# Where the low part of the mixer's weights comes from: a subtraction on GpSimd, or a DMA that adds

## The chip, the core and the metric

One core of a Trainium2 chip runs one inference step of a hybrid decoder layer. The metric is the device time of one execution in microseconds (us). TensorE (PE) multiplies matrices, VectorE (DVE), ScalarE (ACT) and GpSimd (POOL) work element by element, SyncE (SP) only issues DMAs. GpSimd and ScalarE can issue DMAs as well.

## The reference, cut to what matters

The layer is a half-step feed-forward block, a mixer, and a second half-step block, in float32, for 512 prompt tokens and 32 sample tokens (544 columns):

```
x = x + 0.5 * swiglu(rms(x), w_ffn1_gu, w_ffn1_down)
u = rms(x) @ w_in                      # one projection for everything below
o_a = dilated window attention of u's q, k, v   # 12 heads, 3 groups
o_b = gated delta rule of u's q, k, v           # 8 heads, causal convolution before, chunked form
x = x + (sigmoid(gA) * (o_a @ w_proj_a) + sigmoid(gB) * (o_b @ w_proj_b)) @ w_out
x = x + 0.5 * swiglu(rms(x), w_ffn2_gu, w_ffn2_down); y = rms(x)
```

What this case touches is only how the weights of `w_in` come to TensorE, not what is computed with them.

## The kernel before, in words

**Precision.** TensorE reads a short form of float32 (`fp32r`). So each operand is split in two: `hi` is the value rounded to that form, `lo` what is left, value - hi. A product is made of three matmuls, hi x hi, hi x lo and lo x hi, which add up in one PSUM bank.

**Weights.** All weight matrices are cut into 1896 tiles of 128 x 128, laid out in DRAM in the order in which they are used (`Plan`, `in_W_dram`). Four tiles are a group; two groups are a chunk of 512 KB. `load_raw` (line 401) brings a chunk into one of two `raw` buffers; in the mixer it does so from GpSimd's queue (`RQ="gpsimd"`), in the feed-forward blocks from SyncE's. `split_next` (line 424) makes a group out of half a chunk, in a tile `G` of shape 128 x 2 x 512: ScalarE copies `raw` into the first half (`hi`, rounding it), then VectorE or GpSimd writes raw - hi into the second half (`lo`). GpSimd does so in the mixer, except where the unit under way is of kind `pa` or `pb`. `prefetch` (line 457) is called before each unit and splits up to four groups ahead, as far as there are free slots. The mixer has four slots of tag `G`: a column of eight tiles takes two, so while one column is used the next one is made, in the slots of the one before.

**Units.** The program is a list of units (`make_plan`), each a column of up to eight weight tiles times one half of the tokens (272 columns of activations): 24 matmuls (`unit`, line 582) into one PSUM bank `mm`, two units for a column. Within a tile the matmuls are hi x `xh`, hi x `xl`, lo x `xh`; so the third matmul of a unit is the first that needs `lo`. After a unit's matmuls its results are taken out by VectorE (multiplied by the token's 1/rms), and by ScalarE where a tanh follows.

**The mixer.** Its units are the projections: `gdn` (convolution and delta rule, 24 columns), `at` (attention, 36 columns), `z` and `gate`. They are 76 pairs of groups, 152 groups in all. Among them run side chains, written as generators: the causal convolution (tiles `U` and `y`; three VectorE steps y = U * w + y over 568 columns, with a ScalarE step before and a tanh after them), the delta rule for pairs of heads, the attention per slot, and the sample tokens. GpSimd also works for these: small copies of the ends of `U` into `convout`, products of 128 x 512 for the delta rule, and clearing of tiles.

**What sets the order.** The program is written in one order for all engines, and each engine runs its own instructions in that order. A planner decides where the steps of the side chains go: `Meter` keeps an estimate of when each engine gets through what it was given, and `pump` (line 620), called after each weight tile of a unit, issues the side steps that it holds ready. An instruction of GpSimd or a DMA on its queue is counted there with a duration of its own, and a matmul is held to start when its `G` tile is ready.

Of the kernel before, what the change touches and what calls it, by code (L numbers as in the profile page):

```python
# [13 lines left out]
AF = mybir.ActivationFunctionType  # L14
ALU = mybir.AluOpType
AX = mybir.AxisListType

P = 128
# [19 lines left out]
CFG = dict(S=62, S2=4, G=4, G2=8, RAW=2, U3=3, H=10, HM=6, LA=4, LAG=3.0, SLACK=0.0, BANKS=3, PRE=3, LOV=("pa", "pb"), CV=0, WARM=4, EP=8, DUE=2, RES=0, RQ="gpsimd")  # L38
# [7 lines left out]
class Meter:  # L46
    """An estimate of when each engine gets through what it was given, in us.
    It only decides in which order independent work is issued."""
# [77 lines left out]
class Plan:  # L126
    """Order in which the 128 x 128 weight tiles are used; host and chip follow it."""
# [16 lines left out]
def stagger(n, tail, head=0):  # L144
    """(tile, half) order: the first `head` and the last `tail` tiles go half by half."""
    out = [(i, h) for h in range(2) for i in range(head)]
    for i in range(head, n - tail):
        out += [(i, 0), (i, 1)]
    out += [(i, h) for h in range(2) for i in range(n - tail, n)]
    return out  # L150
# [53 lines left out]
def consts():  # L204
    """Arrays that depend on shapes alone: identity, masks and distances."""
# [53 lines left out]
class Builder:  # L259
# [20 lines left out]
    def room(self, keeps):  # L280
        """Tiles that the delta-rule chains under way will still ask for."""
        return max([v for v in self.rest.values() if keeps or v < 16], default=0)

    def need(self, n, keeps=False, room=None, spare=0):
        """Wait, in the order of issue, until n tiles of the common pool are free."""
# [4 lines left out]
    def until(self, ok):  # L290
        """The side chains go on until something holds."""
# [29 lines left out]
    def ring(self, tag, bufs, t):  # L321
        """A tile waits for the one whose place it takes."""
# [65 lines left out]
    def rsqrt(self, out, v, tmp, steps):  # L388
        """out = v ** -0.5 by a shifted exponent and Newton steps."""
# [34 lines left out]
    def split_next(self, ui, pool=None):  # L424
        """Bring the next group of weight tiles in as hi + lo if a slot is free."""
# [19 lines left out]
        self.tt(t[:, 1, :], src, t[:, 0, :], ALU.subtract, self.nc.gpsimd if pool else None)  # L445
# [101 lines left out]
    def xw_tile(self, n, h, which):  # L547
        """x * w as hi + lo; the tokens' 1/rms is applied to the products."""
# [10 lines left out]
    def norm_fin(self, h):  # L559
        """1/rms of one half of the tokens, on all partitions."""  # L560
# [38 lines left out]
    def step(self, g):  # L599
        """One step of a side chain; it says what its next step waits for."""  # L600
# [15 lines left out]
    def pump(self):  # L616
        """Issue what the side chains have ready."""
# [18 lines left out]
    def force(self):  # L636
        """The chain that can go on first goes on."""
# [31 lines left out]
    def run_d(self):  # L669
        """Norms whose sums had time to come together."""  # L670
# [37 lines left out]
    def after_x(self, n, h, which):  # L708
        """The n-th tile of the residual is final: prepare what the next norm needs."""
# [78 lines left out]
    def z_fin(self, n, h, z, t):  # L788
        """A head's output, gated, as hi + lo."""
# [13 lines left out]
    def z_load(self, n):  # L803
        """The output of head n, once it is there."""
# [8 lines left out]
    def fin_a(self):  # L813
        """The attention's heads as hi + lo."""
# [94 lines left out]
    def gating(self):  # L909
        """beta, log decay, its sums within a chunk and their exponentials.  # L910
        Columns: h * 4 + chunk, then two for the sample rows (head of four, sequence, step)."""
# [78 lines left out]
    def token_norms(self, ss, k, cols, bk):  # L990
        """ss [128, 2, k]: sums of squares of q and k.  Returns 1/|q| * dk^-0.5 (k columns),
        beta/|k|^2, that times the decay to the chunk's end, |k|."""
# [225 lines left out]
    def stack(self, a, parts):  # L1218
        """Rows (head, 32) of a, as hi (0) and lo (1), with the parts one above the other: [part, 32], head."""
# [189 lines left out]
    def attn_slot(self, j):  # L1409
        """The prompt rows of slot j.  The group without dilation has its tokens in order (a tile of  # L1410
# [383 lines left out]
```

## Time and profile before

| | us |
|---|---|
| median of three runs | 1734.32 |
| the three runs | 1730.17, 1735.02, 1734.32 |
| span of the profiled execution, which is its own time to 0.1 us | 1730.2 |
| TensorE busy in the span | 1656.1 |
| VectorE, ScalarE, GpSimd busy | 1072.3, 573.1, 373.4 |
| mixer (first to last mixer unit, about) | 425 to 1110 |

The profile is one execution. Its table by stage gives for each stretch of time what each engine was busy; what is missing to the stretch's length is idle time. Its waits say on whom an engine waited. A row of the timeline merges neighbouring equal instructions (x2, x3); its first number is the start in us from the span's beginning. In TensorE's rows of a unit, a row of two `xh` matmuls begins with lo x `xh` of one weight tile and goes on with hi x `xh` of the next.

### The profile page before, as it was taken

The page shows a single profiled execution, that of the slowest core. Times are in us where ns is not written, and L with a number is a line of the kernel's source. Part 1 is how long each engine was busy: PE and PEld are TensorE (multiplying, and loading weights), DVE is VectorE, ACT ScalarE, POOL GpSimd, SP SyncE. Part 2 cuts the span into 40 slices and gives each one's busy share as a digit, 9 for nine tenths or more (in the row PEclk, how much of TensorE's full clock was granted, in tenths as well). Part 3 has the DMA queues.
Part 4 walks back from the last instruction along what each step waited for, and adds up shares of the span by engine and source line. Part 5 has one row for each costly group of instructions (what it writes and reads, how often), then busy time and mean ns, then how long its engine had stood idle before and what let it go on. Part 6 is the DMA issues. An engine that isn't in the chain of part 4 may idle for free.

```text
span 1730.2 us, 33573 instructions
## 1 busy us (share of the span) xinstructions
PE 1656.1 (96%) x13373; PEld 1607.8 (93%) x13373; DVE 1072.3 (62%) x2508; ACT 573.1 (33%) x1356; POOL 373.4 (22%) x441
## 2 busy tenths in 40 slices
PE   8999999999988999999899899999999999999997
PEld 7999999999988888888889788999999999999996
DVE  7754255545879869789958665344456654255534
ACT  5332223332332324343333244333233323223332
POOL 5000000011545534454425233420011000000012
PEclk9999999999999999999999999999999999999999
DMA  5223222322333455446347666332243222223221
GB/s 177 87 85 98 86 86 86 98 85 75 111 100 115 135 180 185 135 156 193 117 137 238 171 219 182 123 119 89 86 139 97 84 89 87 97 74 98 86 75 63
DMA packets 116434, 205.13 MB, mean 119 GB/s; under 512 B 30962, under 2 KB 57108, under 8 KB 116276
## 3 DMA queue, kind: packets, MB, share of 16 engines
q1 hardware_dynamic: 104708, 162.43, 29.2%
q0 software_dynamic: 10992, 39.99, 7.7%
q8 instruction: 105, 1.72, 0.4%
q10 hardware_dynamic: 576, 0.56, 0.1%
q14 instruction: 53, 0.43, 0.1%
HBM read 172.20 MB, written 30.73 MB: 117 GB/s over the span
## 4 chain that ended last, share of the span: by engine, by line
PE 73%; DVE 20%; DMA 3%; ACT 2%; issue 2%; SPq 1%; POOL 0%; DVEq 0%; ACTq 0%
PE sd L120 40%; PE mm L120 32%; DVE y L120 4%; DVE Yc L120 3%; DVE inv L120 2%; DVE H L120 1%; DVE nrm L120 1%; DVE ast L120 1%; DVE av L120 1%; DVE s L120 1%; DVE R L120 1%; DMA md<-ast 1%; DVE U L120 1%; DVE kq L120 1%; DVE r L120 1%
## 5 line engine op out<-in xcount | busy, mean ns | idle before, releaser
L120 PE MATMUL mm<-xh,G 128*128 128x272 f32 x3632 | 753.7, 297 | 21.6 <-DVE smp L120 10.4
L120 PEld LDWEIGHTS mm<-xh,G 128*128 128x128 f32 x3632 | 596.6, 192 | 42.5 <-issue 26.5
L120 PE MATMUL mm<-xl,G 128*128 128x272 f32 x1816 | 530.0, 292 | 0.5 <-DVE xl L120 0.4
L120 PE MATMUL sd<-xh,G 128*128 128x272 f32 x1904 | 363.4, 288 | 0.0
L120 PEld LDWEIGHTS mm<-xl,G 128*128 128x128 f32 x1816 | 349.2, 192 | 1.4 <-DVE xl L120 0.6
L120 ACT ACTIVATE G<-raw 128x512 fp32r<-128x512 f32 x474 | 273.3, 619 | 178.6 <-PE mm L120 111.6
L120 PEld LDWEIGHTS sd<-xh,G 128*128 128x128 f32 x1904 | 300.5, 188 | 0.2
L120 POOL TENSOR_TENSOR G<-raw,G 128x512 fp32r<-128x512 f32 x158 | 217.3, 1391 | 322.7 <-ACT G L120 303.0
L120 PE MATMUL sd<-xl,G 128*128 128x272 f32 x952 | 273.8, 288 | 0.0
L120 DVE TENSOR_TENSOR G<-raw,G 128x512 fp32r<-128x512 f32 x316 | 204.7, 690 | 70.9 <-ACT G L120 66.7
L120 POOL TENSOR_TENSOR acc<-acc,H 128x272 f32<-128x272 f32 x55 | 44.7, 814 | 911.5 <-ACT H L120 908.1
L120 PEld LDWEIGHTS sd<-xl,G 128*128 128x128 f32 x952 | 179.0, 188 | 0.1
L120 PE MATMUL sd<-hh,G 128*128 128x272 f32 x1287 | 163.0, 288 | 0.0
L120 PEld LDWEIGHTS sd<-hh,G 128*128 128x128 f32 x1287 | 161.8, 188 | 0.1
L120 ACT ACTIVATE H<-H 128x272 f32<-128x272 f32 (+1 forms) x105 | 45.1, 429 | 193.4 <-DVE H L120 193.4
L120 ACT ACTIVATE hh<-H 128x272 fp32r<-128x272 f32 x88 | 38.0, 431 | 202.0 <-DVE H L120 202.0
L120 PE MATMUL mm<-hh,G 128*128 128x272 f32 x825 | 104.7, 288 | 0.0
L120 PEld LDWEIGHTS mm<-hh,G 128*128 128x128 f32 x825 | 103.8, 188 | 0.0
L120 DVE SCALAR_TENSOR_TENSOR y<-U,vec,y 128x568 f32<-128x568 f32 x72 | 94.2, 1308 | 7.8 <-ACT y L120 6.0
L120 DVE SCALAR_TENSOR_TENSOR H<-H,H 128x272 f32<-128x272 f32 x120 | 55.2, 460 | 26.3 <-ACT H L120 25.8
L120 DVE SCALAR_TENSOR_TENSOR x<-sd,x 128x272 f32<-128x272 f32 x49 | 21.4, 439 | 77.9 <-PE sd L120 77.9
L120 DVE TENSOR_TENSOR hh<-H,hh 128x272 fp32r<-128x272 f32 x88 | 38.9, 442 | 43.8 <-ACT hh L120 43.8
(257 smaller groups left out, 1853.3 us busy)
## 6 DMA issues: line engine op xcount, KB each, us to landing
raw<-in_W_dram SPq DMA_DIRECT2D x161, 512.0 KB, 3.6
raw<-in_W_dram POOLq DMA_DIRECT2D x76, 512.0 KB, 4.0
qkv<-qd SPq DMA_DIRECT2D x36, 256.0 KB, 5.4
st<-in_ssm_dram SPq DMA_DIRECT2D x32, 256.0 KB, 4.5
cache<-in_kc_dram SPq DMA_DIRECT2D x28, 256.0 KB, 5.2
cache<-in_vc_dram SPq DMA_DIRECT2D x28, 256.0 KB, 4.3
qd<-av SPq DMA_DIRECT2D x24, 256.0 KB, 4.2
out_dram<-av SPq DMA_DIRECT2D x24, 256.0 KB, 3.8
```

The costliest lines, as they stand in the source:

```text
L120: r = f(*args, **kw)
```

## The change

In the mixer `split_next` no longer subtracts. ScalarE, after writing `hi`, writes -hi into the `lo` half; then a DMA from GpSimd's queue loads the group's raw weights from DRAM a second time (128 x 512 float32, 256 KB) and adds them onto -hi in place. The `raw` buffer is then read by ScalarE alone. Outside the mixer nothing changes (`DL` is `"mix"`). The rest of the diff removes comments and docstrings.

```
-CFG = dict(S=62, S2=4, G=4, G2=8, RAW=2, ...
+CFG = dict(DL="mix", S=62, S2=4, G=4, G2=8, RAW=2, ...
...
         self.act(t[:, 0, :], src, AF.Copy)
         if pool is None:
             pool = self.in_mix and self.units[ui][0] not in CFG["LOV"]
-        self.tt(t[:, 1, :], src, t[:, 0, :], ALU.subtract, self.nc.gpsimd if pool else None)
+        if CFG["DL"] == "all" and ui >= CFG["EP"] or self.in_mix:
+            self.act(t[:, 1, :], t[:, 0, :], AF.Copy, scale=-1.0)
+            self.nc.gpsimd.dma_start(t[:, 1, :], self.A["in_W_dram"][c][:, o:o + GRP * P], accum_op=ALU.add)
+        else:
+            self.tt(t[:, 1, :], src, t[:, 0, :], ALU.subtract, self.nc.gpsimd if pool else None)
```

GpSimd's queue, near the mixer's start, before: two subtractions, the next raw load, two more, a raw load, the copies of the convolution's ends.

```order
L120 TENSOR_TENSOR G_4915<-raw_4511,G_4915 128x512
L120 TENSOR_TENSOR G_4918<-raw_4511,G_4918 128x512
L120 DMA raw_4921<-in_W_dram 128x1024
L120 TENSOR_TENSOR G_4987<-raw_4824,G_4987 128x512
L120 TENSOR_TENSOR G_4990<-raw_4824,G_4990 128x512
L120 DMA raw_4993<-in_W_dram 128x1024
L120 COPY convout_4653<-U_4950 128x3
L120 COPY convout_4653<-U_4950 128x24
```

The same place after: each subtraction is a DMA into `G`, and the second pair stands behind the copies.

```order
L120 DMA G_4919<-in_W_dram 128x512
L120 DMA G_4923<-in_W_dram 128x512
L120 DMA raw_4927<-in_W_dram 128x1024
L120 COPY convout_4653<-U_4962 128x3
L120 COPY convout_4653<-U_4962 128x24
L120 DMA G_5010<-in_W_dram 128x512
L120 DMA G_5014<-in_W_dram 128x512
L120 DMA raw_5018<-in_W_dram 128x1024
```

The copies were put ahead of the second pair, and every subtraction became an issue of a DMA.

ScalarE at the same place, before (`y` from `U` is the convolution's first step, `U` from `y` its tanh, `G` from `raw` a split):

```order
L120 ACTIVATE G_4918<-raw_4511 128x512
L120 ACTIVATE G_4987<-raw_4824 128x512
L120 ACTIVATE G_4990<-raw_4824 128x512
L120 ACTIVATE U_4856<-y_4913 128x568
L120 ACTIVATE y_5016<-U_4950,vec_79 128x568
L120 ACTIVATE G_5071<-raw_4921 128x512
L120 ACTIVATE G_5074<-raw_4921 128x512
```

And after (`G` from `G` is -hi):

```order
L120 ACTIVATE y_4917<-U_4860,vec_79 128x568
L120 ACTIVATE G_4919<-raw_4511 128x512
L120 ACTIVATE G_4919<-G_4919 128x512
L120 ACTIVATE G_4923<-raw_4511 128x512
L120 ACTIVATE G_4923<-G_4923 128x512
L120 ACTIVATE U_4860<-y_4917 128x568
L120 ACTIVATE y_5008<-U_4962,vec_79 128x568
L120 ACTIVATE G_5010<-raw_4828 128x512
L120 ACTIVATE G_5010<-G_5010 128x512
```

The second pair of splits moved from ahead of the tanh to behind it and behind the next convolution's first step, and each split is two instructions.

ScalarE in the plain run of gate units near the mixer's end, before (`gate` is the tanh that takes out a unit, `oh` a split of the attention's output):

```order
L120 ACTIVATE gate_13471<-gate_13471 128x272
L120 ACTIVATE oh_13481<-oA_13409 128x512
L120 ACTIVATE gate_13471<-gate_13471 128x272
L120 ACTIVATE G_13507<-raw_13370 128x512
L120 ACTIVATE G_13510<-raw_13370 128x512
```

And after:

```order
L120 ACTIVATE gate_13483<-gate_13483 128x272
L120 ACTIVATE oh_13493<-oA_13432 128x512
L120 ACTIVATE gate_13483<-gate_13483 128x272
L120 ACTIVATE G_13519<-raw_13385 128x512
L120 ACTIVATE G_13519<-G_13519 128x512
L120 ACTIVATE G_13523<-raw_13385 128x512
L120 ACTIVATE G_13523<-G_13523 128x512
```

Here nothing moved; the pair of splits became four instructions behind the same tanh.

## Rows read from the trace of the kernel before

**Rows 1.** Table by stage: length, busy us per engine, clock, DMA share, GB/s

```profile
core 0 of [0], span 1730.2 us
core 0: us, PE busy (x) PEld busy (x) DVE busy (x) ACT busy (x) POOL busy (x), PEclk, DMA share, GB/s
0.00:425.00 425.00, 416.17 (x3253) 412.86 (x3254) 233.95 (x448) 139.43 (x292) 35.90 (x42) 0.99 0.29 94
425.00:560.00 135.00, 119.11 (x863) 116.00 (x862) 111.28 (x263) 38.75 (x95) 64.86 (x72) 0.92 0.35 114
560.00:860.00 300.00, 278.69 (x2372) 259.18 (x2371) 256.60 (x708) 111.04 (x308) 134.55 (x171) 0.98 0.50 156
860.00:1020.00 160.00, 148.78 (x1346) 134.68 (x1346) 107.62 (x330) 51.29 (x159) 60.82 (x71) 0.98 0.57 179
1020.00:1110.00 90.00, 85.79 (x723) 79.04 (x722) 49.25 (x132) 36.61 (x96) 33.11 (x36) 0.96 0.65 198
1110.00:1150.00 40.00, 40.00 (x322) 40.00 (x321) 12.60 (x29) 15.98 (x38) 19.35 (x20) 1.00 0.28 92
```

**Rows 2.** TensorE's waits, 425 to 1110 us: who for whom, us, times, longest

```profile
PE mm L120 <- DVE smp L120: 10.4, 3, 5.1
...
PE mm L120 <- ACT G L120: 3.4, 1, 3.4
PE sd L120 <- ACT r L120: 3.4, 1, 3.4
...
PE mm L120 <- POOL G L120: 1.4, 2, 0.8
...
PE mm L120 <- DVE inv L120: 0.2, 1, 0.2
```

**Rows 3.** Instructions on tile raw, 425 to 1110 us: ns min/median/max; landings

```profile
L120 ACT ACTIVATE G<-raw x138: 612/616/651, 434.0 to 1107.5; 128x512 fp32r<-128x512 f32 x138
L120 POOL TENSOR_TENSOR G<-raw,G x138: 1260/1292/1927, 434.7 to 1109.0; 128x512 fp32r<-128x512 f32 x138
L120 POOL DMA_DIRECT2D raw<-in_W_dram x68: 551/562/602, 438.1 to 1098.8; - x68
...
DMA to landing us min/median/max: 3.7/4.1/13.0
```

**Rows 4.** Instructions on tile y: ns min/median/max, first and last start

```profile
L120 DVE SCALAR_TENSOR_TENSOR y<-U,vec,y x72: 792/1516/2996, 434.1 to 853.3; 128x568 f32<-128x568 f32 x72
```

**Rows 5.** Timeline of VectorE at 517 us: start, us, instruction

```profile
516.85 4.32 DVE L120 SCALAR_TENSOR_TENSOR y<-U,vec,y 128x568 f32<-128x568 f32 x3 [0.97 <-ACT y L120]
```

**Rows 6.** Timeline of GpSimd at 517 us

```profile
517.36 3.21 POOL L120 TENSOR_TENSOR G<-raw,G 128x512 fp32r<-128x512 f32 x2 [1.17 <-ACT G L120]
```

**Rows 7.** DMAs of the attention's cache, 256 KB each, and their landing

```profile
L120 SPq DMA_DIRECT2D cache<-in_kc_dram x28: 327/422/1755, 604.8 to 1047.4; - x28
L120 SPq DMA_DIRECT2D cache<-in_vc_dram x28: 365/425/906, 619.4 to 1079.4; - x28
...
DMA to landing us min/median/max: 2.8/4.7/7.9
```

**Rows 8.** The page's DMA issues: count, KB each, median us to landing

```profile
raw<-in_W_dram SPq DMA_DIRECT2D x161, 512.0 KB, 3.6
raw<-in_W_dram POOLq DMA_DIRECT2D x76, 512.0 KB, 4.0
```

**Rows 9.** Timeline of ScalarE in the gate units

```profile
1113.22 1.14 ACT L120 ACTIVATE G<-raw 128x512 fp32r<-128x512 f32 x2
```

**Rows 10.** Timeline of TensorE in the gate units

```profile
1118.48 0.42 PE L120 MATMUL mm<-xh,G 128*128 128x272 f32 x2
```

**Rows 11.** Timeline of ScalarE at 770 us

```profile
770.67 1.13 ACT L120 ACTIVATE G<-raw 128x512 fp32r<-128x512 f32 x2
```

**Rows 12.** Timeline of TensorE at 772 us

```profile
772.69 0.40 PE L120 MATMUL mm<-xh,G 128*128 128x272 f32 x1 [0.84 <-POOL G L120]
```

## What the change will do to the time

> **What bounds the kernel now.** I read the page first, then one table by stage, the waits of TensorE, and then single tiles and stretches. The stages before 425 us and after about 1150 us are the two feed-forward blocks. They are untouched, and TensorE is nearly gapless there: 416.2 of 425 us [rows 1]. Everything happens in the mixer, from 425 to 1110 us. There TensorE is busy 119.1 of 135, 278.7 of 300, 148.8 of 160 and 85.8 of 90 us, so it stands idle for 15.9 + 21.3 + 11.2 + 4.2 = 52.6 us [rows 1]. The granted clock is 0.92, 0.98, 0.98 and 0.96 in these four stretches. A mean below 1 means that part of the time TensorE ran at 1.2 instead of 2.4 GHz; the loss is 0.08 x 135 + 0.02 x 300 + 0.02 x 160 + 0.04 x 90 = 23.6 us. It comes where TensorE had stood idle: the stretch with the largest idle share, 12%, has the lowest clock, and in 1110 to 1150 us, without idle time, it is 1.00 [rows 1]. So a us of idle time in the mixer goes with 23.6 / 52.6 = 0.45 us of lost clock, and I multiply every change of idle time by 1.45.
>
> What ends these waits is mostly VectorE: 18 rows of the table of waits name it, from 10.4 us down to 0.2 us, in sum 39 us; ScalarE ends 7.5 us outside the weights (four rows, the largest 3.4 us). The weights themselves end few: "POOL G" 1.4 us, "ACT G" 3.4 us [rows 2]. So the split of the weights is now nearly hidden, and the mixer is paced by TensorE with VectorE close behind, busy 111 of 135 us and 257 of 300 us in the first two stretches [rows 1].
>
> **What goes.** GpSimd's subtraction, 152 times in the mixer. One lasts 1260 ns at the least and 1292 ns as a median [rows 3]. GpSimd is not a bound, but VectorE suffers beside it: the three-input step on y takes 792 ns at the least, 1516 ns as a median and up to 2996 ns [rows 4]. At 516.85 us three of them take 4.32 us where three times the least would be 2.4 us; GpSimd's pair of subtractions at 517.36 us lies inside, and takes 3.21 us in place of twice 1.26 [rows 5, 6]. Each holds up the other. Summed over the 247 VectorE instructions of the mixer that overlap a subtraction, each against the shortest of its own form, that is 98 us of VectorE time, the largest part of it y. How much of it TensorE sees: for each of its waits on VectorE or ScalarE I took the smaller of the wait and of the stretching inside VectorE's unbroken run just before. The sum is 34 us, the upper end; the lower end is 0, as another input may be late next (a transfer, or ScalarE with its new work). I take 20 us, nearer the upper end, since in most of these waits the stretching exceeds the wait.
>
> The Trainium skill says the same of this conflict: its page "SBUF — State Buffer", section "SBUF: two separate sides", calls the port pair of the two engines an exclusive lock held for a whole instruction. The trace agrees with 792 against 2996 ns [rows 4]. The same page warns that GpSimd, locked out, can't write the descriptors of its own DMAs either; by that, the new transfers would start late where VectorE is busiest, and the slow landing among the rivals would gain weight. The issuing instruction itself shows nothing of it: 551 to 602 ns in 68 cases [rows 3].
>
> **What comes: ScalarE.** One more pass per group, -hi from hi, at the cost of a split: 616 ns [rows 3]. 152 of them are 94 us on an engine that is busy 38.8 of 135 us and 111.0 of 300 us [rows 1]. It is in order, so what stands behind a pair of groups (tanh of the convolution, copies out of PSUM) comes up to 1.2 us later; most of that lies beside VectorE's y, which is longer. I price it at nothing. If that cover fails, what it can cost is bounded by 4 waits of 1.2 us each, 5 us, since four rows of waits on ScalarE are there now.
>
> The planner, too, now counts -hi and a transfer, so the side steps stand elsewhere among the units: one pair of splits that stood ahead of a tanh on ScalarE now stands behind it and behind the next convolution's first step. The list of units stays. What this can do lies within the 39 + 7.5 us of waits on side steps [rows 2]; I set it at nothing, and keep a tenth of them, 5 us, to either side.
>
> **What comes: the transfer.** A 256 KB load with an addition, from GpSimd's queue, in place of 1.3 us of arithmetic. On GpSimd it stands where the subtraction stood, and it waits for ScalarE as that did; behind it in the queue stand the next raw load and the two small copies of U, which were held just as long before. No row shows a transfer that adds. Nearest rows: loads of 256 KB from SyncE's queue land in 2.8 us at the least and 4.7 us as a median, 7.9 at most, in the crowded middle [rows 7]; 512 KB from GpSimd's queue take 3.7, 4.1 and 13.0 us [rows 3]; over the whole run 512 KB take 3.6 us by SyncE and 4.0 by GpSimd [rows 8], so GpSimd's queue costs 0.4 us more. Below: 2.8 + 0.4 = 3.2 us, an addition for free. Above: 5.5 us, twice the 2.8 us. I take 4.3 us: the adding transfer has to read both the weights and -hi, 512 KB, so the 512 KB row (4.1 us) is nearest, and I add 0.2 us for the addition, an estimate.
>
> The Trainium skill has a price of its own, in "DMA: Bandwidth & Descriptors", section "Anatomy of one DMA": 2.0 us and the bytes at 436 GB/s, which is 2.6 us for 256 KB, an estimate that counts no addition. For the plain 512 KB load it gives 3.2 us, and the trace 3.7 at the least [rows 3], so it is low here.
>
> **Who has to wait.** A column of eight weight tiles is two groups. ScalarE begins the first split of a pair at a time H, when it is through with the last work on the unit before; the third matmul of the unit that uses the pair is the first that reads lo. With the change the first lo lands at H + 2 x 0.62 (hi, -hi) + 0.2 (two handovers) + L, thus H + 1.44 + L; the second group's at H + 2.7 + L, but it is wanted 1.5 us later, so the first decides. In the plain run of gate units H is 1113.22 us and the matmul at 1118.48 us, 5.26 us later [rows 9, 10]. In the worst pair it is 770.67 and 772.69 us, 2.02 us [rows 11, 12]. Over the 76 pairs of the mixer (H from ScalarE's rows, units counted through at 24 matmuls): 13 have 2.0 to 4.75 us, 13 have 5.27 to 5.73 us, 50 have more. With L = 4.3 the need is 5.74 us: the first 13 are short by 29 us in sum, the next 13 by 4 us, together 33 us. With L = 3.2 it is 15 us, with 3.7 it is 21 us, with 5.5 it is 69 us. Some of the 13 are late only because ScalarE waited for a stretched y; taking that stretching out of H shortens the 33 us by 5 us.
>
> **Sum.** Idle time: + 33 - 5 - 20 = + 8 us, with the clock 1.45 x 8 = + 12 us. The profiled execution has a span of 1730.2 us [rows 1], which is the lowest of the three runs; the median, 1734.3 us, lies 4 us above. So 1742 us on the profile's scale and 1746 us as a median.
>
> **Rivals.**
> Hidden transfer, on the other side: L is 3.2 to 3.7 us, the loss 15 to 21 us less 3 us, and VectorE's relief the full 34 us. Idle time changes by 18 - 34 = -16 us at 3.7 us and by 12 - 34 = -22 us at 3.2 us; times 1.45, from 1734.3 us, that is 1711 to 1702 us. For it speaks the 2.8 us row; against it that raw loads of GpSimd never landed under 3.7 us. It decides from L below about 3.9 us together with relief above 25 us. The Trainium skill's formula above (2.6 us) would end beyond it: 10 us of loss less 3 us and 34 us, times 1.45, 1695 us.
>
> A wash: relief and loss within 4 us of each other, 1734 us. That needs L near 4 us, or relief near 28 us; both are well inside the bounds.
>
> Slow landing: adding is as slow as two transfers one after the other, or the crowded middle (DMA share 0.50 to 0.65 [rows 1], to which the change adds 152 x 256 KB = 40 MB) pushes the median beyond 5 us. With L = 5.5: 69 - 9 - 20 = + 40 us, times 1.45 = + 58 us, 1792 us. Even the gate units would then wait, 1.7 us for each column.
>
> That the change does not do what it says: the order of the built program has the 152 DMAs on GpSimd's queue and 152 more passes on ScalarE, so this is left without a chance.
>
> **How the numbers follow.** About 0.3% (5 us) can be told from no change. Forecast (L from 4.0 to 5.2 us, 1740 to 1770 us): 0.39. Slow landing: 0.15. Hidden transfer: 0.28. A wash: 0.18. Slower by over 0.3% thus 0.54, the same 0.18, faster 0.28. The range 1712 to 1786 us leaves out the far half of the hidden transfer and most of the slow landing, about 0.2. The forecast's own range is 1740 to 1770 us.
>
> **What would show it.** Right: the landing of G's DMA at 4 to 5 us; y near 0.8 us in all 72 cases; TensorE's waits on a DMA into G at 25 to 40 us, most of them in 425 to 560 and after 1020 us; its waits on VectorE down from 39 to about 20 us; a clock of 0.92 or lower in 425 to 560 us. Wrong: landing under 3.7 us, or no waits on G at all, or y as long as before, in which case the subtraction was not what stretched it.

## The result and the profile after

The changed kernel takes **1827.0 us** in the median (1818.8 to 1830.9), the kernel before 1733.1 on the same chip. The ratio is 1.053, interval 1.050 to 1.056: slower by 92 us. The forecast, 12 us slower, had the sign; the size is more than seven times that, and beyond its range.

The table by stage of the changed kernel (length, busy us per engine, clock, DMA share, GB/s):

```profile
core 0 of [0], span 1817.0 us
core 0: us, PE busy (x) PEld busy (x) DVE busy (x) ACT busy (x) POOL busy (x), PEclk, DMA share, GB/s
425.00:560.00 135.00, 119.75 (x886) 114.93 (x887) 91.70 (x286) 63.22 (x134) 48.52 (x81) 0.97 0.80 191
560.00:860.00 300.00, 252.60 (x2054) 230.79 (x2054) 191.86 (x627) 126.59 (x328) 87.12 (x138) 0.92 0.69 182
860.00:1020.00 160.00, 140.85 (x1182) 127.75 (x1181) 90.53 (x319) 57.99 (x149) 44.90 (x71) 0.88 0.69 185
1020.00:1110.00 90.00, 77.55 (x620) 71.07 (x618) 35.00 (x115) 44.15 (x109) 25.87 (x37) 0.94 0.85 237
1110.00:1200.00 90.00, 76.04 (x632) 70.21 (x632) 33.48 (x93) 40.42 (x94) 18.44 (x25) 0.92 0.66 166
1200.00:1240.00 40.00, 34.72 (x264) 33.19 (x265) 10.91 (x25) 19.78 (x39) 13.69 (x18) 1.00 0.69 146
```

Against [rows 1], TensorE stands idle for 15.25 + 47.40 + 19.15 + 12.45 + 13.96 + 5.28 = 113.5 us from 425 to 1240 us, where it was 52.8 us. The lost clock is 0.03 x 135 + 0.08 x 300 + 0.12 x 160 + 0.06 x 90 + 0.08 x 90 = 59.8 us, where it was 23.6. Together that is 97 us more; the profiled spans differ by 86.8 (the clock is given to two places, which is 4 us either way here). The mixer now ends behind 1200 us, so the last two stretches count. The first stretch, where much was expected, is no worse than before; 560 to 860 us is.

TensorE's waits in 415 to 1240 us (who for whom, us, times, longest; `mm` and `sd` are the PSUM tiles that the matmuls write):

```profile
PE mm L120 <- DMA G<-in_W_dram: 50.9, 38, 8.7
PE sd L120 <- DMA cache<-in_kc_dram: 20.6, 5, 7.9
PE sd L120 <- DMA qkv<-qd: 10.2, 1, 10.2
PE sd L120 <- DVE srz L120: 6.7, 2, 4.1
PE sd L120 <- DVE av L120: 4.0, 3, 2.1
```

A DMA ended 0.8 us of TensorE's waits in the kernel before; now it is 87 us, all such rows added. But only 51 of them are waits on the new transfer; 36 are waits on the attention's cache, on `qkv` and on a state of the delta rule (20.6 + 10.2 + 2.9 + 2.2), loads that the change doesn't touch. The rows of VectorE add up to 20.3 us in 425 to 1110 us, where [rows 2] had 39.1.

The step on `y` (ns min/median/max), against [rows 4]:

```profile
L120 DVE SCALAR_TENSOR_TENSOR y<-U,vec,y x72: 769/810/2535, 430.7 to 892.7; 128x568 f32<-128x568 f32 x72
```

The median is down from 1516 to 810 ns. The new transfer, its issue on GpSimd (ns) and its landing (us):

```profile
L120 POOL DMA_DIRECT2D G<-in_W_dram x152: 844/861/940, 432.1 to 1235.7; - x152
...
DMA to landing us min/median/max: 3.6/5.6/9.8
```

And the page's DMA issues (count, KB, median us to landing), against [rows 8]:

```profile
raw<-in_W_dram SPq DMA_DIRECT2D x161, 512.0 KB, 3.6
G<-in_W_dram POOLq DMA_DIRECT2D x154, 256.0 KB, 5.7
raw<-in_W_dram POOLq DMA_DIRECT2D x76, 512.0 KB, 7.0
```

The page counts 154 new transfers: 152 for what GpSimd subtracted, two for groups that VectorE had subtracted. Of all the rows the last was least expected: the plain load beside the new transfer went from 4.0 to 7.0 us.

The median of the new transfer hides two kinds. Matched one by one in the trace, the first of each pair of groups lands in 4.6 us, the second in 6.1 us (77 of each); those issued with no other load of GpSimd's queue still in the air land in 4.5 us (38 transfers). Of TensorE's waits on the transfer, 36 us were ended by the landing of a first group and 15 us by that of a second one.

### The profile page after: what moved, and what is told of

The parts are those of the page before. It is cut to its first block, busy times and chain, and to the rows that moved or that the text cites. A ratio compares the mean times of both kernels' runs of the same rounds, so it can differ in the third digit from the quotient of the medians.

```text
span 1817.0 us, 33826 instructions
## 1 busy us (share of the span) xinstructions
PE 1681.6 (93%) x13373; PEld 1623.9 (89%) x13373; DVE 985.5 (54%) x2506; ACT 670.2 (37%) x1510; POOL 298.2 (16%) x443
## 4 chain that ended last, share of the span: by engine, by line
PE 70%; DMA 14%; DVE 7%; issue 5%; ACT 3%; SPq 1%; DVEq 0%; POOL 0%; ACTq 0%; POOLq 0%
PE sd L120 39%; PE mm L120 31%; DMA G<-in_W_dram 6%; DMA cache<-in_kc_dram 3%; ACT G L120 1%; DVE R L120 1%; DMA md<-ast 1%; SPq L120 1%; DMA cache<-in_vc_dram 1%; DVE H L120 1%; ACT junk L120 1%; DVE Yc L120 1%; DMA st<-in_ssm_dram 1%; DMA Y<-yd 1%; DVE nrm L120 1%
## 5 line engine op out<-in xcount | busy, mean ns | idle before, releaser
L120 PE MATMUL mm<-xh,G 128*128 128x272 f32 x3632 | 763.6, 300 | 54.0 <-DMA G<-in_W_dram 48.3
L120 ACT ACTIVATE G<-raw 128x512 fp32r<-128x512 f32 x474 | 278.8, 619 | 157.1 <-PE mm L120 99.7
L120 POOL DMA_DIRECT2D G<-in_W_dram x154 | 132.9, 863 | 476.0 <-ACT G L120 328.0
L120 ACT ACTIVATE G<-G 128x512 fp32r<-128x512 f32 x154 | 97.3, 632 | 4.9
L120 DVE SCALAR_TENSOR_TENSOR y<-U,vec,y 128x568 f32<-128x568 f32 x72 | 60.9, 846 | 10.1 <-ACT y L120 8.4
L120 POOL DMA_DIRECT2D raw<-in_W_dram x76 | 66.0, 869 | 0.0
```

The source lines that it names most:

```text
L120: r = f(*args, **kw)
```

## The experiments

All have the units in the same sequence and the same matmuls (e7, e8 and e11 turn their order within a unit). "Old bookings" means that the planner counts each group as the kernel before does, whatever is really issued, so that the order on TensorE, VectorE and SyncE is the old one; "new bookings" likewise. The planner's class gets a switch `mute` for this. The traces bear it out: apart from the instructions that make the low part, every engine of e2, e5 and e16 has the sequence of the kernel before (up to two swapped neighbours on VectorE), and every engine of e1, e3 and e4 that of the changed kernel. Each ratio is against runs of the kernel before on the same chip; the last column is (ratio - 1) x 1734 us.

| kernel | bookings | low part by | median us | ratio, interval | us |
|---|---|---|---|---|---|
| before | old | GpSimd | 1734 | 1 | 0 |
| e5 | old | none | 1674.6 | 0.965 (0.963 to 0.967) | -61 |
| e2 | old | adding DMA | 1766.4 | 1.016 (1.012 to 1.021) | +28 |
| e1 | new | GpSimd | 1786.8 | 1.029 (1.024 to 1.034) | +50 |
| e4 | new | none | 1734.5 | 0.998 (0.995 to 1.000) | -4 |
| e3 | new | plain DMA | 1785.7 | 1.028 (1.023 to 1.033) | +49 |
| after | new | adding DMA | 1827.0 | 1.053 (1.050 to 1.056) | +92 |

In e3, `lo` holds the raw weights; e4, e5, e9 and e17 leave the low part of the weights out of the result. They show times, not versions to use.

### Work and order apart

**e1, the new order with the old work:**

```
+            m.mute = True
+            m.gpsimd.tensor_tensor(t[:, 1, :], src, t[:, 0, :], op=ALU.subtract)
+            m.mute = False
+            m.note("scalar", "activation", (t[:, 1, :], t[:, 0, :]), {})
+            m.note("gpsimd", "dma_start", (t[:, 1, :], self.A["in_W_dram"][c][:, o:o + GRP * P]), {})
-            self.act(t[:, 1, :], t[:, 0, :], AF.Copy, scale=-1.0)
-            self.nc.gpsimd.dma_start(..., accum_op=ALU.add)
```

> The order of every engine's instructions is that of the changed kernel, but GpSimd subtracts as before: no -hi pass, no adding DMA. Two theories of the 94 us. Transfers: the adding DMAs cost it, by landing late and by delaying the other DMAs; then this runs like the kernel before, 1715 to 1750 us, and TensorE's waits on DMAs into cache and qkv (36 us in the changed kernel) are near 1 us again. Order: the planner's new places for the side steps cost it; then those waits stay and the time is 1770 to 1800 us.

**e2, the old order with the new work** (the two new lines muted, the subtraction noted in their place):

```
+            m.mute = True
             self.act(t[:, 1, :], t[:, 0, :], AF.Copy, scale=-1.0)
             m.gpsimd.dma_start(..., accum_op=ALU.add)
+            m.mute = False
+            m.note("gpsimd" if pool else "vector", "tensor_tensor", (t[:, 1, :], src, t[:, 0, :]), {})
```

> The order is that of the kernel before, with the work of the changed kernel: ScalarE writes -hi, a DMA on GpSimd's queue adds. Transfers: 1800 to 1830 us, with waits on G's DMA of 40 to 60 us and waits on other DMAs of 20 us or more. Order: waits on G's DMA alone, 1750 to 1780 us.

**e4, the new order, -hi written, nothing transferred:**

```
-            self.nc.gpsimd.dma_start(..., accum_op=ALU.add)
+            self.nc.note("gpsimd", "dma_start", (t[:, 1, :], self.A["in_W_dram"][c][:, o:o + GRP * P]), {})
```

> The changed kernel without the adding DMA: lo stays -hi, which leaves the low part of the weights out of the result. Order and ScalarE's passes are unchanged. This is what VectorE's relief alone is worth, with no transfer against it. Transfers: 1695 to 1715 us, no waits on cache or qkv above 3 us in sum. Order: those waits stay at 20 us or more and the time is 1735 us or more.

**e5, the same in the old order** (e2 without its `dma_start`):

> The order of the kernel before on every engine, ScalarE writes -hi, nothing is transferred and nothing is subtracted, so lo stays -hi: the low part of the weights is left out of the result, the matmuls are all there. It is the change's ceiling in the old order: all relief, no transfer. If the relief of VectorE and GpSimd that the prediction took as 20 us is right, 1710 us with the clock in 560 to 1020 us a little up, and then the transfer in the old order costs 1766 - 1710 = 56 us. If GpSimd's subtraction costs VectorE nothing on the path, about 1738, and the transfer costs 28. The new order with the same work ran in 1734.5 (order and -hi, no transfer); if the new order costs 49 us whatever the work, this kernel should take 1686.

The table gives each of three steps twice or three times. Taking the subtraction away is worth 61 us in the old order (e5) and 50 + 4 = 54 in the new (e1 to e4). Adding the transfer costs 28 + 61 = 89 us in the old order and 92 + 4 = 96 in the new. The new order costs 50 us with the subtraction, 57 with neither, 64 with the transfer. Each step has nearly the same price on whichever other work it is tried: the differences, 7 to 14 us, are about as large as the intervals allow. So they can be added: -61 + 89 + 64 = +92 us. The times expected of the order as the cause came in e1, in e2 and, within 1 us, in e4; e5 came out below all three numbers that were expected for it.

The table by stage of e5, first four stretches:

```profile
425.00:560.00 135.00, 131.79 (x1046) 130.57 (x1045) 101.47 (x317) 75.44 (x168) 22.78 (x56) 1.00 0.45 140
560.00:860.00 300.00, 293.36 (x2669) 272.64 (x2669) 219.11 (x760) 152.72 (x400) 54.23 (x108) 1.00 0.56 168
860.00:1020.00 160.00, 155.44 (x1305) 142.76 (x1304) 96.47 (x316) 78.79 (x193) 23.10 (x42) 0.98 0.68 209
1020.00:1110.00 90.00, 87.18 (x723) 84.11 (x722) 34.34 (x90) 47.39 (x98) 6.12 (x12) 1.00 0.40 125
```

Idle time is 17.2 us against 52.8 before, and the clock is at 1.00 nearly throughout: 3.2 us are lost in place of 23.6. VectorE is busy 219 us in 560 to 860 us in place of 257, ScalarE 153 in place of 111, and TensorE's waits on ScalarE (8.4 us) are no longer than before (10.9). So the -hi pass, 94 us of ScalarE, costs nothing that can be seen. What went are the waits on VectorE: 8.7 us in place of 39.7 from 415 to 1240 us, which is most of the 36 us of idle time; the waits on the weights, on ScalarE's or GpSimd's part of `G`, were 4.8 us and are 2.6, so weights that are ready earlier are not what e5 wins by. Its step on `y`:

```profile
L121 DVE SCALAR_TENSOR_TENSOR y<-U,vec,y x72: 787/810/1468, 432.2 to 805.8; 128x568 f32<-128x568 f32 x72
```

TensorE's waits of e2, the largest three:

```profile
PE mm L121 <- DMA G<-in_W_dram: 53.6, 35, 7.8
PE sd L121 <- ACT r L121: 9.6, 2, 5.0
PE sd L121 <- DMA cache<-in_kc_dram: 7.6, 1, 7.6
```

Idle time is 84.4 us, 67 more than in e5, and 54 of these are the wait on the transfer itself: 37 us on a first group of a pair, 17 us on a second. Those of e1, which has no new transfer:

```profile
PE sd L121 <- DMA cache<-in_kc_dram: 18.7, 4, 10.0
PE sd L121 <- DVE av L121: 11.4, 3, 4.7
PE sd L121 <- DVE srz L121: 9.9, 5, 3.0
```

And those of e4, which has none either:

```profile
PE sd L121 <- DMA cache<-in_kc_dram: 15.8, 4, 8.6
PE sd L121 <- DVE av L121: 6.6, 3, 2.9
PE sd L121 <- DVE srz L121: 6.1, 5, 3.5
```

The waits on the cache and on late side steps thus come with the order alone. All rows added, e4 has 22 us of waits on DMAs and 26 us on VectorE where e5, with the same work, has none and 8.7 us.

### What adding costs against copying

**e3**: the changed kernel without `accum_op=ALU.add`.

> The changed kernel with the same DMA as a plain copy: it does not add, so lo holds the raw weights and the outputs are those of other weights. If the addition makes the transfer long (a packet of 2048 bytes takes 178 ns against 84 ns for plain ones on another queue), the landing falls from 5.8 us to about 4.5 us, G's waits from 51 to under 25 us, and the time to 1765 to 1790 us. If the issue on GpSimd and the second read of the weights do it, the landing stays above 5.3 us and the time above 1800 us.

Issue and landing of the plain transfer:

```profile
L120 POOL DMA_DIRECT2D G<-in_W_dram x152: 527/527/647, 432.6 to 1201.4; - x152
...
DMA to landing us min/median/max: 2.7/3.9/10.8
```

It lands in 3.9 us, the adding one in 5.6, and its issue takes 527 ns of GpSimd against 861. TensorE's waits on it are 36.6 us: the time lies in the range that was expected for the addition as the cause, the waits stayed above the 25 us expected with it. Against e4 the plain transfer costs 53 us and the adding one 96. So of the transfer's price a little more than half is there for any second load of the weights, and 43 us (10 either way) is the addition.

### What in the planner's bookings spoils the order

Three things are booked anew: -hi on ScalarE, the transfer's time on the planner's clocks of GpSimd and of the DMA queues, and the weights' readiness, which in the planner holds for the whole tile, hi and lo: 1.0 + 0.65 + 0.73 + 0.9 = 3.3 us after GpSimd gets to it, where a subtraction is booked at 1.23 us (these are the planner's constants, no measured times).

**e6**, the changed kernel with the planner's DMA clock put back:

```
+            was = self.nc.t["dma"]
             self.nc.gpsimd.dma_start(..., accum_op=ALU.add)
+            self.nc.t["dma"] = was
```

> The changed kernel's work, but the planner's own clock of the DMA queues is put back after each adding transfer is booked; -hi on ScalarE and the readiness of G stay booked as in the changed kernel. Of the 49 us of the new order alone, this asks how much comes from side steps and cache loads being put later because the planner believes the queues taken. Theory A (the shared DMA clock moves the cache loads): the waits on cache (20.6 us) and on qkv (10.2) go, time 1766 to 1785. Theory B (the order changes because the weights are booked as ready later and ScalarE as busier): nothing is won, 1815 to 1830, waits on cache within 5 us of the changed kernel's.

Measured: 1813.9 us, ratio 1.046 (1.043 to 1.049), 12 us better than the changed kernel. Neither theory's number is met exactly, but B is close. TensorE's waits:

```profile
PE mm L120 <- DMA G<-in_W_dram: 53.1, 35, 6.1
PE sd L120 <- DMA cache<-in_kc_dram: 17.7, 5, 12.3
PE sd L120 <- DMA qkv<-qd: 10.5, 1, 10.5
```

The waits on the cache and `qkv` stay: the planner's DMA clock is not what puts these loads late.

**e9**, the work of e4 with -hi and a subtraction booked:

```
             self.act(t[:, 1, :], t[:, 0, :], AF.Copy, scale=-1.0)
-            self.nc.gpsimd.dma_start(..., accum_op=ALU.add)
+            self.nc.note("gpsimd" if pool else "vector", "tensor_tensor", (t[:, 1, :], src, t[:, 0, :]), {})
```

> The work of the two kernels without a transfer (ScalarE writes -hi, nothing is transferred or subtracted, so the low part of the weights is left out of the result): 1674.6 us with the bookings of the kernel before, 1734.5 us with those of the changed one. Here the planner books the -hi pass on ScalarE, as the changed kernel does, and GpSimd's subtraction, as the kernel before does, but no transfer. Theory A: the order goes wrong because ScalarE is booked busier by 94 us: 1720 to 1740 us. Theory B: it goes wrong because a transfer is booked, which makes the weights ready some 2 us later for the planner, so that it believes TensorE's own clock to be later and lets side steps go before their inputs are there: 1674 to 1690 us.

Measured: 1683.5 us, ratio 0.970 (0.967 to 0.973), 8 us above e5. Theory B: the -hi on ScalarE explains 8 of the 57 us, the booked transfer the rest.

**e17**, the work of e4 with all its bookings except the late readiness (after e4's `note`):

```
+            g = t[:, 1, :].tensor.name
+            m.ready[g] = m.used[g] = (m.t["gpsimd"] + 0.23, "gpsimd")
```

> The work without a transfer (ScalarE writes -hi, no subtraction, the low part of the weights is left out of the result), in an order of its own: the planner books -hi and the transfer, with the time of GpSimd and of the DMA queues that it takes, but counts the weights as ready 1.23 us after GpSimd gets to them, as a subtraction would have them, in place of some 3.3 us. The same work took 1674.6 us with the bookings of the kernel before, 1683.5 with -hi booked and 1734.5 with all that the changed kernel books. If the late readiness is what spoils the order: 1675 to 1695 us. If GpSimd's and the queues' booked time spoil it, or any other order than the old one does: 1720 to 1740 us.

Measured: 1671.1 us, ratio 0.961 (0.960 to 0.963), at least as fast as the old order and a little below the range expected for late readiness. Two stretches of its table by stage:

```profile
560.00:860.00 300.00, 294.40 (x2684) 274.94 (x2683) 230.27 (x791) 155.88 (x416) 56.18 (x112) 1.00 0.56 170
860.00:1020.00 160.00, 151.28 (x1254) 138.80 (x1253) 95.11 (x301) 81.04 (x193) 24.06 (x43) 0.98 0.72 211
```

So it is the booked readiness, and with it gone another order than the old one is just as good. That the planner, believing TensorE held up at each group, sends side steps and cache reads to TensorE ahead of their inputs is my reading of `pump` and of the waits on `av`, `srz` and the cache; no run shows it step by step. Nor does the booking help where the lateness is real: with the adding transfer, where the weights do come late, the same order costs 64 us. Early readiness together with the real transfer was not run.

### What the transfer costs: late groups, or the number of transfers

All of these have the old bookings.

**e7 and e8**: in each unit the matmuls with hi first, those with lo last; e7 with the adding transfer, e8 with the subtraction.

```
-        for i, wi in enumerate(wids):
-            hi, lo = self.w(wi)
-            xh, xl = rhs[i][0][:, s], rhs[i][1][:, s]
-            self.mm(ps, hi, xh, i == 0, False)
-            self.mm(ps, hi, xl, False, False)
-            self.mm(ps, lo, xh, False, i == m - 1)
+        seq = [(i, 0, x) for i in range(m) for x in range(2)] + [(i, 1, 0) for i in range(m)]
+        for k, (i, part, x) in enumerate(seq):
+            self.mm(ps, self.w(wids[i])[part], rhs[i][x][:, s], k == 0, k == 3 * m - 1)
```

> The work of the change with the bookings of the kernel before, and in every unit the matmuls with hi run first, for all of the unit's four weight tiles, and those with lo last. The first lo of a group is then needed some 2 us later after the group is there than with hi, hi, lo by turns. Theory (the loss is a transfer that lands 5.6 us after its issue against a need of 2 to 5.7 us): the waits on the DMA of G fall from 53.6 us (old order, adding transfer) to 10 to 20, and the time from 1766 to 1710 to 1735. Rival (the loss is queueing: the adding transfers and the raw loads hold back each other and all other loads, so a group is late however it is read): the waits on G stay over 35 us and the time over 1750.

> The kernel before with the same turn of the matmuls in a unit, hi first and lo last, GpSimd subtracting: the control of the run beside it. If the turn alone is worth nothing in the kernel before, 1738 within 10 us; if the subtraction on GpSimd was itself late for the first lo, up to 15 us less. The weights change once per matmul either way, except that the two matmuls with the same hi stay side by side.

Measured: e7 1755.6 us, ratio 1.012 (1.008 to 1.016); e8 1737.6 us, ratio 1.002 (1.000 to 1.003). The turn is worth nothing by itself. With the transfer it is 7 us from e2 to e7, with an uncertainty of 10 us, so no gain is shown. The theory was too hopeful, and the time falls on the rival's side (over 1750 us), though the wait is below the rival's 35 us:

```profile
PE mm L121 <- DMA G<-in_W_dram: 30.8, 23, 5.3
```

So 23 us of waiting on the transfer went, but other waits took part of the place (DVE `as` 8.6 us where e2 had 3.9).

**e10 and e11**: the second group of each pair by transfer, the first by subtraction; e11 with lo last as well.

```
+            if pool and k % 2:
                 self.act(t[:, 1, :], t[:, 0, :], AF.Copy, scale=-1.0)
                 m.gpsimd.dma_start(..., accum_op=ALU.add)
+            else:
+                self.tt(t[:, 1, :], src, t[:, 0, :], ALU.subtract, m.gpsimd if pool else None)
```

> Order and bookings of the kernel before. Of each pair of groups the first, which is wanted first, has its low part from GpSimd's subtraction, the second from -hi and the adding transfer: 76 transfers and 76 subtractions in place of 152 of one kind. If what the transfer costs in the old order (1766 - 1675 = 91 us) comes from groups that are late for their first matmul with lo, most of it falls on the first of a pair and goes, and half of the relief of 60 us stays: 1705 to 1735 us, waits on the DMA of G under 20 us. If the transfers cost by their number, through the queue and the slower transfers beside them, half of each: 1734 - 30 + 46 = 1750 us.

> As the run beside it, and in every unit the matmuls with hi run first and those with lo last, which put off the first lo by some 2 us. If lateness of the low part is what is left there, it goes, and the relief shows: 1695 to 1720 us, waits on the DMA of G under 8 us. If the run beside it has no waits on G worth naming, the two are within 10 us of each other.

Measured: e10 1731.3 us, ratio 0.999 (0.997 to 1.001); e11 1730.9, ratio 0.997 (0.995 to 1.000). Half the transfers are nearly free, but they win nothing either; the waits on them are longer than theory A had them (under 20 and under 8 us), and lo last, which takes 10 us of them away, doesn't show in the time. The waits on the transfer in e10:

```profile
PE mm L121 <- DMA G<-in_W_dram: 24.4, 9, 5.8
```

and its DMA issues:

```profile
raw<-in_W_dram POOLq DMA_DIRECT2D x76, 512.0 KB, 6.4
G<-in_W_dram POOLq DMA_DIRECT2D x76, 256.0 KB, 4.3
```

A transfer without a partner just ahead of it lands in 4.3 us, and still 24 us are waited for these second groups.

And in e11:

```profile
PE mm L121 <- DMA G<-in_W_dram: 14.9, 6, 4.5
```

**e12, e13 and e14**: the condition is `if pool and k in BY_DMA:`, with the groups chosen by how long after the start of their first split the first matmul with lo came, in the trace of the kernel before. e12: the 77 with 8 us or more; e13: the 75 with less; e14: the 100 with 6.5 us or more.

> Order and bookings of the kernel before. Of the 152 groups, the 77 whose first matmul with lo came 8 us or more after their first split began, in the trace of the kernel before, get their low part from -hi and the adding transfer, the other 75 by GpSimd's subtraction. Theory A (a transfer costs where the group is late for that matmul, and nothing else): waits on the DMA of G under 6 us, half of the relief stays, 1700 to 1712 us. Theory B (transfers cost by their number, by delaying the other loads and by holding GpSimd's queue): 1734 - 30 + 46 = 1750 us; the run with every second group of a pair gave 1731.

> The other half: the 75 groups with less than 8 us by the adding transfer, the 77 with more by subtraction. Theory A: all of the lateness is here, the 91 us of the old order less the half of the relief, 1734 - 30 + 80 to 91 = 1784 to 1795 us, waits on the DMA of G 45 to 55 us. Theory B: as the run beside it, near 1750 us.

> As the first of these runs with the bound at 6.5 us: 100 groups by transfer. By theory A two thirds of the relief stay (40 us) and a few groups are late, since -hi, handover and a landing of 4.3 to 5.6 us need 5.7 to 7.1 us: 1695 to 1710 us. By theory B 1755 us.

Measured: e12 1727.2 us, ratio 0.997 (0.995 to 0.998); e13 1750.7, ratio 1.010 (1.007 to 1.012); e14 1727.3, ratio 0.996 (0.994 to 0.998). The waits on the transfer in e12:

```profile
PE mm L125 <- DMA G<-in_W_dram: 10.8, 9, 3.3
```

And in e13:

```profile
PE mm L125 <- DMA G<-in_W_dram: 43.9, 25, 6.6
```

Equal numbers of transfers, 22 us apart, and four fifths of the waiting on the short half: lateness is a real part. But e12 stayed well above theory A, and e13 well below its 1784 us; e13 landed on theory B's number and e12 did not. If half of the relief (30 us) is in each, the long half costs 30 - 5 = 25 us and the short half 30 + 17 = 47, together 72 of the 89. That each half has its share is borne out by TensorE's waits on VectorE: 19.0 us in e12, 20.9 in e13, 39.7 before. So neither theory holds alone. That the long half pays by the number of transfers is not shown: the largest new wait in e12 is again the one on the transfer, 10.8 us. Its DMA issues:

```profile
raw<-in_W_dram POOLq DMA_DIRECT2D x76, 512.0 KB, 6.1
G<-in_W_dram POOLq DMA_DIRECT2D x77, 256.0 KB, 5.6
```

The plain load took 4.0 us before. One by one, the 35 of e12's plain loads that were issued with no transfer in the air land in 4.0 us, the 31 with two in the air in 7.1 us. So the landing goes with what is right ahead in GpSimd's queue, more than with how many transfers there are in all. Even with the best choice found, the transfers win 7 us.

### The subtraction on VectorE

**e16**: the kernel before, old bookings, all 152 subtractions on VectorE. **e15**: e14, with its other 52 groups on VectorE.

```
-                self.tt(t[:, 1, :], src, t[:, 0, :], ALU.subtract, m.gpsimd if pool else None)
+                self.tt(t[:, 1, :], src, t[:, 0, :], ALU.subtract)
```

> The kernel before with all 152 subtractions of the mixer on VectorE in the place in its order where GpSimd had them, without transfers. It asks what the stretching is worth: 152 x 0.69 = 105 us more for VectorE against the 98 us that GpSimd's subtractions stretch it by. If the stretching is an even exchange, 1725 to 1745 us, y at 0.8 us throughout. If the quicker subtraction also takes waits away, 1700 to 1720. If VectorE becomes the bound in 425 to 860 us, above 1750.

> As the run with 100 groups by transfer (those with 6.5 us or more in the trace of the kernel before), but the other 52 groups are subtracted by VectorE, 0.69 us each, so that GpSimd does no arithmetic on the weights at all. Order and bookings of the kernel before. If what is left of the stretching of VectorE there (y up to 2.3 us) is the rest of the relief, and VectorE has room for 36 us more, 1700 to 1720 us. If VectorE in its order of issue, waiting for a split or a raw load, holds its side steps up, 1730 to 1760 us, with TensorE's waits on VectorE above 25 us.

Measured: e16 **1719.0 us**, ratio 0.990 (0.986 to 0.994), the fastest complete version; e15 1732.8, ratio 0.998 (0.996 to 1.000). In e16 the page has VectorE busy for 1070.0 us, against 1072.3 before: 105 us of added subtraction are paid by the stretching that goes. Its step on `y`:

```profile
L121 DVE SCALAR_TENSOR_TENSOR y<-U,vec,y x72: 790/810/1742, 436.9 to 843.1; 128x568 f32<-128x568 f32 x72
```

its subtraction:

```profile
L121 DVE TENSOR_TENSOR G<-raw,G x144: 670/684/695, 426.8 to 1107.6; 128x512 fp32r<-128x512 f32 x144
```

and two stretches of its table by stage:

```profile
425.00:560.00 135.00, 124.25 (x920) 121.11 (x919) 109.54 (x324) 42.63 (x101) 18.25 (x45) 0.95 0.39 119
560.00:860.00 300.00, 283.52 (x2406) 263.91 (x2405) 249.16 (x763) 108.60 (x304) 51.85 (x109) 0.97 0.54 164
```

TensorE is busy 5 us more in each than in [rows 1]. The even exchange was the first guess; the quicker subtraction (0.68 us in place of 1.29) is an extra. So of the 61 us that e5 wins, 17 come from moving the work off GpSimd, and 44 more only from not doing it. In e15 the waits on VectorE stay small (16.6 us in all, no row over 4.9), so VectorE is not held up by its new work; the transfers take their price again. Its largest wait is

```profile
PE mm L126 <- DMA G<-in_W_dram: 20.5, 12, 4.1
```

## Why the prediction was wrong, point by point

**The planner's new order** is the step that failed and took the result out of the range. The prediction saw that the planner counts -hi and a transfer, and wrote "I set it at nothing, and keep a tenth of them, 5 us, to either side". It measured 50 to 64 us, in three pairs of kernels, and without it the result would have stayed in the range (e2, 1766 us). The bound was taken from the waits of before, 46.5 us; but waits that the old order doesn't have (36 us on loads that the change doesn't touch, in the profile after) can't be read there. The prediction bounded a new order by the old order's waits; the thing to price was the booked number that moves it, 3.3 us in place of 1.23 us for each of 152 groups.

**The landing and who waits** is the second step that failed, inside a term that was mis-sized. The landing was set at 4.3 us and measured 5.6 us as a median, beyond the upper bound of 5.5. Yet for a transfer with nothing ahead of it the figure was right: 4.3 us in e10, and 4.6 us for the first of each pair in the changed kernel. The waits on first groups, 36 to 37 us, are close to the 33 us that were forecast. What failed is "so the first decides": behind its partner the second group's transfer lands in 6.1 us, 1.5 us later than the first, and 15 to 17 us more are waited for it. The prediction put the same landing on both. The plain load behind the pair is late in the same way (7.0 us in place of 4.0). The whole transfer cost 89 us in the old order, against 1.45 x (33 - 5) = 41 us forecast. The slow landing, a rival with a chance of 0.15, gives nearly the measured price (with L = 5.5, 69 us of lateness, less 9, times 1.45 = 87 us), but by 60 us of waiting where 54 are measured and with every transfer at 5.5 us; that agreement is luck.

**The relief** was set at 20 us of idle time with an upper end of 34. e5 against before: 52.8 - 17.2 = 35.6 us of idle time, and 61 us of time, since the clock came back whole. The upper end was the right value. It was refused because "another input may be late next"; in e5 the rows of waits name no other input that grew. VectorE's busy time fell by 96 us (1072.3 to 975.9), where 98 us of stretching was summed.

The Trainium skill, in "SBUF — State Buffer", section "SBUF: two separate sides", which the prediction weighed, calls the shared port an exclusive lock; e16 agrees as far as it goes: with the same subtractions on VectorE its busy time doesn't rise, and `y` stands at 810 ns in the median. The same page warns that GpSimd, locked out while VectorE runs an operation in a two-port mode, can't write the descriptors of its DMAs. The issuing instructions show no sign of it, 844 to 940 ns in 152 cases; whether it would show there or in the landings, 3.6 to 9.8 us, no run tells apart.

**ScalarE at nothing**: right. Waits on ScalarE are 8.4 us in e5 against 10.9. (The 5 us bound counted four rows of waits, which are five waits.)

**The factor 1.45** from idle time to time: right in size for the whole: idle time rose by 60.7 us and the profiled span by 86.8, a factor of 1.43. It is no rule for a single stretch: 425 to 560 us has 15.9 us of idle time before and 15.3 after, and the granted clock is 0.92 and 0.97. In e5, 3.2 us of lost clock stand beside 17.2 us of idle time, 0.19 in place of 0.45.

**The sum.** In its own terms the forecast was + 33 - 5 - 20 + 0 idle us. The runs say, in us of time: transfer +89, relief -61, order +64. Times 1.45 the forecast had +41, -29 and 0. So the transfer and the relief were both set at less than half of what they measured, and that their difference (+28 us, e2) lies inside the range is luck: two errors of about the same size cancel. The order, at nothing, took the result out of it.

**What was to show it.** `y` at 0.8 us: in the median, not in all 72 (longest 2.5 us; 2.3 in e4, without transfers). TensorE's waits on VectorE down to about 20 us: 20.3. Waits on the transfer 25 to 40 us: 51, of which 10 in 415 to 560 us and 28 behind 1020 us, so the places were right. The clock at or below 0.92 in 425 to 560 us: 0.97 there, but 0.92 and 0.88 in the two stretches behind, where the idle time went.

## What to carry to other kernels

When an edit also feeds a planner, run it twice: with the new work booked as the old, and with the old work booked as the new. Here that split showed two effects of some 60 us that the total hides, and that one constant (when a tile counts as ready) costs as much as the whole edit can win.

A second load of the same bytes has to be priced with what stands right ahead of it in its queue, and the loads behind it too, each against the time until its first reader. And where two engines stretch each other, try the work on the stretched engine as well: 105 us of subtraction left VectorE's busy time as it was here.

## What the runs showed of the hardware

- A DMA that adds is not a plain one with a small surcharge: 256 KB land in 5.6 us in place of 3.9 (at the least 3.6 in place of 2.7), and GpSimd spends 861 ns on an issue in place of 527. The issues of the plain loads between them take 876 ns too (535 in e3, 562 before), so the longer issue is not of the adding instruction alone. The packets are the same in number; one of the adding transfer (2048 bytes) takes 178 ns in the median, one of the plain copy in e3 99 ns. The software queue, which carries the plain loads as well, in the changed kernel (packets, MB, share of 16 engines):

```profile
q0 software_dynamic: 33168, 80.37, 19.9%
```

And of e3:

```profile
q0 software_dynamic: 33168, 80.37, 15.7%
```

- What follows it in the queue lands later: plain 512 KB loads issued by GpSimd land in 7.0 us behind adding transfers, 5.3 behind plain ones (e3), 4.0 without [rows 8]; a second adding transfer behind a first lands in 6.1 us in place of 4.6. The plain load's own packets (4096 bytes) take 159 ns in the median in all three, which speaks for a load that waits, not for one that moves more slowly.
- The clock of TensorE came back more fully than expected: with 17 us of idle time in 815 us (e5, e17) it was granted 1.00 in five of six stretches; with 47 us in 300 us (the changed kernel) 0.92, a mean of times at 2.4 and at 1.2 GHz. Idle time alone does not fix it: 15.9 and 15.3 us in 425 to 560 us go with 0.92 and 0.97.
